# Weights of all gemms split by two GpSimd loads, one rounding and one adding, in place of one SyncE load, a ScalarE rounding and a VectorE subtraction

## The chip, the cores and the metric

One core of one Trainium2 chip runs the whole program. The metric is the device time of one execution in microseconds (us); lower is better. The engines are TensorE (PE, its weight loads PEld), VectorE (DVE), ScalarE (ACT), GpSimd (POOL) and SyncE (SP). SP, ACT and POOL can issue DMA transfers; all of these run on the core's 16 DMA engines.

## The reference, cut to what matters

Two blocks run on 512 tokens of width 1024 in fp32. The first has two layers (a mixer of two linear recurrences, then a gated feed-forward with a convolution), the second one layer (four mixers, then an MLP).

```python
def first_block(x, ...):
    for l in range(DEPTH):                      # 2 layers
        h = _rmsnorm(x, mix_norm[l])
        x = x + _mixer(h, w_in[l], ..., w_branch_dn[l], w_branch_hg[l], w_out[l])
        h = _rmsnorm(x, ffn_norm[l])
        x = x + _conv_ffn(h, w_up[l], ffn_conv[l], ffn_conv_bias[l], w_down[l])
    return _rmsnorm(x, final_norm)

def _mixer(h, w_in, ...):
    p = h @ w_in                                # 1024 x 6672
    ...                                         # gated delta rule and HGRN2, 4 heads each, both directions
    merged = (jax.nn.sigmoid(gate_dn) * (o_dn @ w_branch_dn)
              + jax.nn.sigmoid(gate_hg) * (o_hg @ w_branch_hg))
    return merged @ w_out

def _conv_ffn(h, w_up, ffn_conv, ffn_conv_bias, w_down):
    gate, up = _split(h @ w_up, (D_FF, D_FF))   # D_FF = 2816
    gate = _dwconv(gate, ffn_conv) + ffn_conv_bias
    return (jax.nn.silu(gate) * up) @ w_down

def second_block(x, ...):                       # one layer
    ...
    mixed = jnp.sum(gates * proj, axis=2)       # gates: 1024 x 4096, proj: four branches 256 x 1024
    x = x + jnp.einsum('bsd,de->bse', mixed, w_out[l])
    hn = _rms(x, norm2_g[l])
    hid = jnp.square(jax.nn.relu(jnp.einsum('bsd,df->bsf', hn, w_mlp1[l])))   # 1024 x 4096
    x = x + jnp.einsum('bsf,fd->bsd', hid, w_mlp2[l])
    return x
```

## The kernel before

Activations are kept with features on the partitions, tokens (512) along the row. Every product with a weight matrix goes through `gemm` (L264). Weights lie in HBM in blocks of 128 output columns; a block of 8 chunks of 128 inputs is a tile [128, 8, 128], 512 KB. To keep fp32 precision with matmuls on fp32r operands (a float format of the same size with a rounded mantissa), both operands are split into a rounded high half and a low half: the product is hi·xh + hi·xl + lo·xh, three matmuls of 128x512 for each chunk, so 24 for a block, added up in one PSUM bank `pd` (two banks).

`weights` (L235) makes the halves. SP loads the raw block `wr` (L244, three buffers), ACT writes its rounding `wh` (L245, two buffers), DVE writes `wl` = raw - hi (L246, two buffers). `mm3` (L249) issues the three matmuls of a chunk (L257). The activation's halves `xh`, `xl` are made by `split` (L276).

The order on each engine is written by a scheduler that plays the program through a model of its times; what comes out is a fixed order on each engine, with semaphore waits between engines. In the first block's mixers (`mixer`, L718) the gemms of `w_in` are mixed with the recurrences of the heads: `gdn_front`, `gdn_inverse`, `gdn_scan` (L435 to L612), and `hg_head` (L631), whose loop over seven doublings runs over PE (`ph`, L682), DVE (`att` L684, `qk` L686) and POOL (`pq` L687). After them come the branch products and `w_out` (L774 on), the feed-forward (`ffn`, L784: 44 blocks of `w_up`, of which every second one is followed by a POOL product `fs` L803, then 8 gemms of 22 chunks with `w_down`), and in the second block `mixer2` (L1084) and `mlp` (L1129). POOL carries elementwise work of the recurrences and eight small transfers (`k2`, L961, L962); it issues no weight loads.

Of the kernel before, what the change touches and what calls it, by code (L numbers as in the profile page):

```python
# [17 lines left out]
P = 128  # L18
# [155 lines left out]
class Net:  # L174
# [59 lines left out]

    def weights(self, src, lo="v", small=None):  # L235
        nc = self.nc
        n, c = src.shape[1], src.shape[2]
        pl, k, bf = (self.wp, 8, (3, 2, 2)) if small is None else (small, 2, (2, 2, 2))
        raw, hi, lw = (pl.tile([P, k, P], dt, name=self.nmx(t), tag=t, bufs=b) for t, dt, b in zip(("wr", "wh", "wl"), (F32, F32R, F32R), bf))
        if c == P:  # L240
            raw, hi, lw = raw[:, :n], hi[:, :n], lw[:, :n]
        else:
            raw, hi, lw = (t.rearrange("p a b -> p (a b)")[:, :n * c].rearrange("p (a b) -> p a b", b=c) for t in (raw, hi, lw))
        nc.sync.dma_start(raw, src)  # L244
        nc.scalar.activation(hi, raw, AF.Copy)  # L245
        (nc.vector if lo == "v" else nc.gpsimd).tensor_tensor(lw, raw, hi.bitcast(F32), op=ALU.subtract)  # L246
        return hi, lw
# [6 lines left out]
    def mm(self, *a, **k):  # L254
        """a matmul; those of a paced stretch are queued behind the steps of a scan, a few after each"""
        if not self.pace:
            return self.nc.tensor.matmul(*a, **k)  # L257
        with self.tc.issue_after(self.pace[0]):
            self.nc.tensor.matmul(*a, **k)  # L259
        self.paced += 1  # L260
        if self.paced % PACE == 0:
            self.pace.pop(0)

    def gemm(self, srcs, xs, lo="v", m=P):  # L264
        bank = self.bank("pd")
        ps = bank[:m]
        nk = sum(s.shape[1] for s in srcs)
        k = 0
        for s in srcs:
            hi, lw = self.weights(s, lo)  # L270
            for i in range(s.shape[1]):
                self.mm3(ps, hi[:, i], lw[:, i], xs[k][0], xs[k][1], k == 0, k == nk - 1)
                k += 1
        return bank
# [52 lines left out]
    def norm2_end(self, st):  # L327
        """the final norm of the first block and the first of the second in one"""
        nc = self.nc
# [67 lines left out]
    def gdn_small(self, l, xs, rb, sp):  # L397
        """token-major gates of all heads: columns (c, d*4+h)"""
        nc = self.nc
# [77 lines left out]
    @staticmethod  # L477
    def pair(t, width, b, first, off, n):
        """columns off .. off + n of a tile [P, 2 * width], blocks of b taken in turn from its halves, from half `first` at the start"""
        return bass.AP(tensor=t.tensor, offset=t.offset + off + first * width, ap=[list(t.ap[0]), [2 * b, n // (2 * b)], [b + (1 - 2 * first) * width, 2], [1, b]])  # L480
# [340 lines left out]
    def gemm_tok(self, w, xs, n, rb, pool, tmp, tag):  # L821
        """a bank [tokens, 4, n]"""
        t = self.evac(self.gemm([w], xs, m=n)[:n], rb[:n], pool, *tmp, part=n)
# [5 lines left out]
    def fold_final(self):  # L829
        """fin * norm1 gains, used while the last FFN of the first block leaves"""  # L830
        self.fg = self.cp.tile([P, KD], F32, name="fg1")
        self.nc.vector.tensor_tensor(self.fg, self.col("fin", 0, 8), self.col("n1", 0, 8), op=ALU.mult)
# [321 lines left out]
def place_tables(nc):  # L1154
    """Loads of activation tables, each for the longest run of functions that one set serves"""
    from concourse.hw_specs import get_activation_tables
# [63 lines left out]
```

## Time and profile before

| | |
|---|---|
| three runs | 2740.33, 2744.57, 2746.9 us; median 2744.57 us |
| profiled execution | span 2742.3 us from the first to the last instruction; its own time is not listed apart from the span |
| busy share of the span | PE 96%, PEld 79%, DVE 57%, ACT 41%, POOL 12% |
| mean granted TensorE clock | 0.983 of full speed |
| HBM read | 238.36 MB, of which the weights by SP's queue 215.17 MB |
| weight blocks | 449 loads by SP; 449 ACT roundings; 449 DVE subtractions |

The span is the time on the chip between the first and the last instruction. A busy share is a mean over stages that differ; a PE that is busy may still run below its full rate, since the ends of matmuls are modelled.

### The profile page before, as it was taken

The page shows a single profiled execution, that of the slowest core. Times are in us where ns is not written, and L with a number is a line of the kernel's source. Part 1 is how long each engine was busy: PE and PEld are TensorE (multiplying, and loading weights), DVE is VectorE, ACT ScalarE, POOL GpSimd, SP SyncE. Part 2 cuts the span into 40 slices and gives each one's busy share as a digit, 9 for nine tenths or more (in the row PEclk, how much of TensorE's full clock was granted, in tenths as well). Part 3 has the DMA queues.
Part 4 walks back from the last instruction along what each step waited for, and adds up shares of the span by engine and source line. Part 5 has one row for each costly group of instructions (what it writes and reads, how often), then busy time and mean ns, then how long its engine had stood idle before and what let it go on. Part 6 is the DMA issues. An engine that isn't in the chain of part 4 may idle for free.

```text
span 2742.3 us, 32455 instructions
## 1 busy us (share of the span) xinstructions
PE 2645.3 (96%) x12674; PEld 2178.6 (79%) x12674; DVE 1556.6 (57%) x2234; ACT 1124.7 (41%) x1511; POOL 329.2 (12%) x282
## 2 busy tenths in 40 slices
PE   7999899999999979998999999999999999999999
PEld 4788788878888857887888788888777788888887
DVE  6778764455554366778644555534874444553442
ACT  6545544343333255455443433333446443332221
POOL 1112320001110011122200011100100111000000
PEclk9999989999999999999999999999999999999999
DMA  4112212253223332111123423234411232433332
GB/s 149 62 49 67 62 39 68 88 167 100 94 98 114 121 89 70 55 61 54 39 76 101 160 95 100 93 121 127 145 64 51 82 96 94 140 129 99 94 104 88
DMA packets 99064, 254.13 MB, mean 93 GB/s; under 512 B 10016, under 2 KB 31520, under 8 KB 98656
## 3 DMA queue, kind: packets, MB, share of 16 engines
q1 hardware_dynamic: 66960, 215.17, 24.5%
q10 hardware_dynamic: 31568, 35.85, 4.5%
q8 instruction: 100, 1.64, 0.2%
q0 software_dynamic: 384, 1.05, 0.1%
q14 instruction: 52, 0.43, 0.1%
HBM read 238.36 MB, written 12.62 MB: 92 GB/s over the span
## 4 chain that ended last, share of the span: by engine, by line
PE 49%; ACT 1%; DVE 0%; issue 0%; POOL 0%; ACTq 0%; DVEq 0%; POOLq 0%
PE pd L257 45%; PE ph L1065 1%; PE pl L1053 1%; PE pd L259 1%; ACT wh L245 0%; PE pr L1061 0%; ACT L1179 0%; PE pl L972 0%; PE ph L682 0%; PE pl L843 0%; DVE wl L246 0%; ACT rb L294 0%; ACT rb L295 0%; PE pl L1015 0%; PE ph L1039 0%
## 5 line engine op out<-in xcount | busy, mean ns | idle before, releaser
L257 PE MATMUL pd<-xh,wh 128*128 128x512 f32 (+1 forms) x3186 | 1265.8, 398 | 36.3 <-DVE raw L449 14.3
L257 PE MATMUL pd<-xh,wl 128*128 128x512 f32 (+1 forms) x3188 | 1258.0, 395 | 2.6 <-DVE wl L246 2.3
L257 PE MATMUL pd<-xl,wh 128*128 128x512 f32 (+1 forms) x3186 | 1253.7, 394 | 2.1 <-DVE xl L290 2.0
L245 ACT ACTIVATE wh<-wr 128x1024 fp32r<-128x1024 f32 (+5 forms) x449 | 434.9, 969 | 1011.3 <-PE pd L257 866.8
L257 PEld LDWEIGHTS pd<-xh,wh 128*128 128x128 f32 (+1 forms) x3186 | 600.2, 188 | 178.8 <-issue 20.9
L257 PEld LDWEIGHTS pd<-xl,wh 128*128 128x128 f32 (+1 forms) x3186 | 600.3, 188 | 139.2 <-issue 7.2
L257 PEld LDWEIGHTS pd<-xh,wl 128*128 128x128 f32 (+1 forms) x3188 | 600.0, 188 | 138.7 <-DVE wl L246 5.0
L246 DVE TENSOR_TENSOR wl<-wr,wh 128x1024 fp32r<-128x1024 f32 (+5 forms) x449 | 521.7, 1162 | 250.3 <-ACT wh L245 244.1
L1179 ACT ACT_TABLE_LOAD x116 | 148.8, 1283 | 8.7 <-issue 4.4
L394 DVE TENSOR_TENSOR g<-pd,rb 128x512 f32<-128x512 f32 x64 | 44.3, 692 | 158.2 <-PE pd L257 148.1
L803 POOL TENSOR_TENSOR fs<-fs,rb 128x512 f32<-128x512 f32 x44 | 56.9, 1294 | 506.3 <-ACT fs L802 506.3
L682 PE MATMUL ph<-pq,kc 128*128 128x128 f32 x448 | 74.8, 313 | 19.6 <-POOL er L569 6.7
L797 DVE TENSOR_TENSOR fg<-pd,rb 128x512 f32<-128x512 f32 x44 | 30.5, 693 | 109.9 <-PE pd L257 107.0
L682 PEld LDWEIGHTS ph<-pq,kc 128*128 128x128 f32 x448 | 66.7, 213 | 26.4 <-issue 19.2
L687 POOL TENSOR_TENSOR pq<-pq,f 128x512 f32<-128x512 f32 x48 | 58.8, 1225 | 230.7 <-PE ph L682 211.5
L805 DVE TENSOR_TENSOR fs<-fs,pd 128x512 f32<-128x512 f32 x44 | 30.3, 688 | 90.0 <-POOL fs L803 90.0
L801 DVE SCALAR_TENSOR_TENSOR fs<-fg,cv,fs 128x512 f32<-128x512 f32 x88 | 65.9, 749 | 3.6 <-ACT fs L799 1.9
L802 ACT ACTIVATE fs<-fs 128x512 f32<-128x512 f32 x44 | 27.8, 632 | 85.5 <-DVE fs L801 85.5
L394 DVE TENSOR_TENSOR mh<-pd,rb 128x512 f32<-128x512 f32 x32 | 22.1, 692 | 70.2 <-PE pd L257 68.8
L680 ACT COPY kc<-qk 128x512 f32<-128x512 f32 x56 | 36.9, 659 | 52.2 <-PE ph L682 44.5
L454 DVE SCALAR_TENSOR_TENSOR qk<-raw,cv,qk 128x512 f32<-128x512 f32 x64 | 54.1, 858 | 2.6 <-ACT qk L452 2.2
L684 DVE COPY_PREDICATED att<-um,ph 128x512 f32<-128x512 uint8 x56 | 41.2, 736 | 21.5 <-PE ph L682 21.2
(332 smaller groups left out, 2442.5 us busy)
## 6 DMA issues: line engine op xcount, KB each, us to landing
wr<-in_w_in_dram SPq DMA_DIRECT2D x126, 512.0 KB, 3.3
wr<-in_w_up_dram SPq DMA_DIRECT2D x88, 512.0 KB, 3.3
wr<-in_w_m_dram SPq DMA_DIRECT2D x64, 512.0 KB, 3.8
wr<-in_w_dn_dram SPq DMA_DIRECT2D x32, 512.0 KB, 3.6
wr<-in_w_gt_dram SPq DMA_DIRECT2D x32, 512.0 KB, 3.3
wr<-in_w_out_dram SPq DMA_DIRECT2D x24, 512.0 KB, 3.4
xd<-xn ACTq DMA_DIRECT2D x40, 256.0 KB, 2.0
xo<-xd ACTq DMA_DIRECT2D x32, 256.0 KB, 2.8
```

What stands on the lines that cost most here:

```text
L245: nc.scalar.activation(hi, raw, AF.Copy)
L246: (nc.vector if lo == "v" else nc.gpsimd).tensor_tensor(lw, raw, hi.bitcast(F32), op=ALU.subtract)
L257: return self.nc.tensor.matmul(*a, **k)
L394: self.nc.vector.tensor_tensor(out, ps, rb, op=ALU.mult)
L454: V.scalar_tensor_tensor(o, raw[:, j:j + T], self.col(f"dnc{l}_{j}", ch), o, op0=ALU.mult, op1=ALU.add)
L680: A.copy(kc.rearrange("p (n e b) -> p n e b", e=2, b=hh), self.pair(qk, T, hh, 0, 0, T))
L682: PE.matmul(pl[:, c], kc[:, c * P:(c + 1) * P], self.pair(pq, T, hh, 1, c * P, P), start=True, stop=True)
L684: V.copy_predicated(att, self.um[:, o:o + P].unsqueeze(1).to_broadcast([P, 4, P]), pl)
L687: (G if hh > 1 else V).tensor_tensor(halves(pq, hh, True), halves(pq, hh, True), tot(F, n, 0, n + 1, hh), op=ALU.mult)
L801: nc.vector.scalar_tensor_tensor(g, gp[:, j:j + T], self.col(f"fc{l}_{j}", m), g, op0=ALU.mult, op1=ALU.add)
L803: nc.gpsimd.tensor_tensor(g, g, rb, op=ALU.mult)
L1179: nc.scalar.preload_act_table_set(s)
```

## The change

The high half is loaded by GpSimd straight into the fp32r tile `wh` (four buffers), so that the transfer rounds. ACT writes its negative into `wl` (three buffers), and a second GpSimd transfer of the same block adds the raw weights to it: -hi + raw. The raw tile, SP's load and the DVE subtraction go. In `gemm`, the 16 matmuls of a block that use the high half come first, then the 8 of the low half. The small weights of the second block's branches (`small`, two chunks) get three buffers each and keep the old order of matmuls.

```diff
-    def weights(self, src, lo="v", small=None):
+    def weights(self, src, small=None):
...
-        pl, k, bf = (self.wp, 8, (3, 2, 2)) if small is None else (small, 2, (2, 2, 2))
-        raw, hi, lw = (pl.tile([P, k, P], dt, name=self.nmx(t), tag=t, bufs=b) for t, dt, b in zip(("wr", "wh", "wl"), (F32, F32R, F32R), bf))
+        pl, k, bf = (self.wp, 8, (4, 3)) if small is None else (small, 2, (3, 3))
+        hi, lw = (pl.tile([P, k, P], F32R, name=self.nmx(t), tag=t, bufs=b) for t, b in zip(("wh", "wl"), bf))
...
-        nc.sync.dma_start(raw, src)
-        nc.scalar.activation(hi, raw, AF.Copy)
-        (nc.vector if lo == "v" else nc.gpsimd).tensor_tensor(lw, raw, hi.bitcast(F32), op=ALU.subtract)
+        nc.gpsimd.dma_start(hi, src)
+        nc.scalar.activation(lw, hi.bitcast(F32), AF.Copy, scale=-1.0)
+        nc.gpsimd.dma_start(lw, src, accum_op=ALU.add)
         return hi, lw
...
-        for s in srcs:
-            hi, lw = self.weights(s, lo)
-            for i in range(s.shape[1]):
-                self.mm3(ps, hi[:, i], lw[:, i], xs[k][0], xs[k][1], k == 0, k == nk - 1)
-                k += 1
+        for j, s in enumerate(srcs):
+            hi, lw = self.weights(s)
+            n = s.shape[1]
+            for i in range(n):
+                self.mm(ps, hi[:, i], xs[k + i][0], start=j == 0 and i == 0, stop=False)
+                self.mm(ps, hi[:, i], xs[k + i][1], start=False, stop=False)
+            for i in range(n):
+                self.mm(ps, lw[:, i], xs[k + i][0], start=False, stop=j == len(srcs) - 1 and i == n - 1)
+            k += n
```

On POOL, in the first head's doubling loop in the first mixer, the order before has the six products `pq` one after the other (what a row waits for stands in brackets):

```order
L687 TENSOR_TENSOR pq_768<-pq_768,f_159_923 128x2x128x2 [waits DVE_49,PE_49]
L687 TENSOR_TENSOR pq_768<-pq_768,f_766 128x2x64x4 [waits DVE_49,PE_49,Pool_49]
L687 TENSOR_TENSOR pq_768<-pq_768,f_159_923 128x2x32x8 [waits DVE_49,PE_49,Pool_49]
L687 TENSOR_TENSOR pq_768<-pq_768,f_766 128x2x16x16 [waits DVE_49,PE_49,Pool_49]
L687 TENSOR_TENSOR pq_768<-pq_768,f_159_923 128x2x8x32 [waits DVE_49,PE_49,Pool_49]
L687 TENSOR_TENSOR pq_768<-pq_768,f_766 128x2x4x64 [waits DVE_49,PE_49,Pool_49]
```

The same place of the changed program (the line of `pq` is now L691; L245 is the rounding load, L247 the adding one):

```order
L691 TENSOR_TENSOR pq_761<-pq_761,f_148_912 128x2x128x2 [waits DVE_49,PE_49]
L245 DMA wh_1594<-in_w_in_dram 128x1024 [waits DMASW3_49,PE_49]
L691 TENSOR_TENSOR pq_761<-pq_761,f_759 128x2x64x4 [waits DVE_49,PE_49,Pool_49]
L247 DMA wl_1558<-in_w_in_dram 128x1024 [waits DMASW6_49,Activation_49]
L245 DMA wh_1627<-in_w_in_dram 128x1024 [waits DMASW5_49,PE_49]
L691 TENSOR_TENSOR pq_761<-pq_761,f_148_912 128x2x32x8 [waits DVE_49,PE_49,Pool_49]
L247 DMA wl_1595<-in_w_in_dram 128x1024 [waits DMASW0_49,Activation_49]
L691 TENSOR_TENSOR pq_761<-pq_761,f_759 128x2x16x16 [waits DVE_49,PE_49,Pool_49]
L245 DMA wh_1791<-in_w_in_dram 128x1024 [waits DMASW7_49,PE_49]
L691 TENSOR_TENSOR pq_761<-pq_761,f_148_912 128x2x8x32 [waits DVE_49,PE_49,Pool_49]
L247 DMA wl_1628<-in_w_in_dram 128x1024 [waits DMASW2_49,Activation_49]
L691 TENSOR_TENSOR pq_761<-pq_761,f_759 128x2x4x64 [waits DVE_49,PE_49,Pool_49]
```

Three loads of each kind now stand between these products; a load of `wh` waits for PE (its buffer), one of `wl` for ACT (the negative).

On POOL in the first layer's `w_up`, the order before holds only the products `fs`, one for two blocks:

```order
L803 TENSOR_TENSOR fs_4726<-fs_4726,rb_4673 128x512 [waits Activation_49]
L803 TENSOR_TENSOR fs_4800<-fs_4800,rb_4673 128x512 [waits Activation_49]
L803 TENSOR_TENSOR fs_4874<-fs_4874,rb_4673 128x512 [waits Activation_49]
L803 TENSOR_TENSOR fs_4948<-fs_4948,rb_4673 128x512 [waits Activation_49]
L803 TENSOR_TENSOR fs_5022<-fs_5022,rb_4673 128x512 [waits Activation_49]
```

The changed program has there (a block's `wl` has the number of its `wh` plus one):

```order
L807 TENSOR_TENSOR fs_4792<-fs_4792,rb_4596 128x512 [waits Activation_49]
L247 DMA wl_4907<-in_w_up_dram 128x1024 [waits DMASW6_49,Activation_49]
L245 DMA wh_4978<-in_w_up_dram 128x1024 [waits DMASW5_49,PE_49]
L247 DMA wl_4944<-in_w_up_dram 128x1024 [waits DMASW0_49,Activation_49]
L245 DMA wh_5015<-in_w_up_dram 128x1024 [waits DMASW7_49,PE_49]
L807 TENSOR_TENSOR fs_4864<-fs_4864,rb_4596 128x512 [waits Activation_49]
L247 DMA wl_4979<-in_w_up_dram 128x1024 [waits DMASW2_49,Activation_49]
```

The adding load of a block stands one place behind the rounding load of the next block, and four loads stand between two products.

On PE in the same stretch, the order before alternates the halves within each chunk:

```order
L257 MATMUL pd_5176<-xh_4494,wh_5178 128x512
L257 MATMUL pd_5176<-xl_4495,wh_5178 128x512
L257 MATMUL pd_5176<-xh_4494,wl_5179 128x512
L257 MATMUL pd_5176<-xh_4537,wh_5178 128x512
L257 MATMUL pd_5176<-xl_4538,wh_5178 128x512
L257 MATMUL pd_5176<-xh_4537,wl_5179 128x512
```

The changed order, at the place in a block where its low half begins:

```order
L258 MATMUL pd_5086<-xl_4548,wh_5087 128x512
L258 MATMUL pd_5086<-xh_4589,wh_5087 128x512
L258 MATMUL pd_5086<-xl_4590,wh_5087 128x512
L258 MATMUL pd_5086<-xh_4297,wl_5088 128x512 [waits DMASW6_49]
L258 MATMUL pd_5086<-xh_4337,wl_5088 128x512
L258 MATMUL pd_5086<-xh_4379,wl_5088 128x512
```

The first low-half matmul moved from third to seventeenth in its block and waits for the adding load itself; the number of matmuls is the same.

## Rows read from the trace of the kernel before

**Rows 1.** The page: span, then busy time, share and instructions of each engine.

```profile
span 2742.3 us, 32455 instructions
PE 2645.3 (96%) x12674; PEld 2178.6 (79%) x12674; DVE 1556.6 (57%) x2234; ACT 1124.7 (41%) x1511; POOL 329.2 (12%) x282
```

**Rows 2.** Busy time by stretch, columns as headed: two mixers, one feed-forward's `w_up`.

```profile
core 0: us, PE busy (x) PEld busy (x) DVE busy (x) ACT busy (x) POOL busy (x), PEclk, DMA share, GB/s
0.00:450.00 450.00, 405.31 (x2224) 340.19 (x2225) 319.57 (x531) 235.70 (x320) 91.92 (x83) 0.95 0.22 68
...
605.00:843.00 238.00, 237.50 (x1045) 195.69 (x1044) 126.09 (x152) 92.48 (x113) 28.47 (x22) 1.00 0.30 97
...
1000.00:1400.00 400.00, 360.24 (x2054) 310.29 (x2054) 289.45 (x458) 198.86 (x266) 90.83 (x67) 0.94 0.19 57
```

**Rows 3.** What PE waited for, 0 to 450: total us, times, longest.

```profile
PE ph L698 <- DVE att L684: 4.4, 2, 3.4
...
PE ph L682 <- POOL er L569: 3.5, 1, 3.5
...
PE pd L257 <- DVE wl L246: 0.3, 1, 0.3
```

**Rows 4.** What PE waited for, 1000 to 1400.

```profile
PE pd L257 <- DVE raw L449: 10.4, 1, 10.4
...
PE ph L682 <- POOL er L569: 3.2, 1, 3.2
...
PE pr L589 <- DVE zf L550: 0.4, 1, 0.4
```

**Rows 5.** Groups by line over the whole span: busy, mean ns, idle before.

```profile
L245 ACT ACTIVATE wh<-wr 128x1024 fp32r<-128x1024 f32 (+5 forms) x449 | 434.9, 969 | 1011.3 <-PE pd L257 866.8
...
L246 DVE TENSOR_TENSOR wl<-wr,wh 128x1024 fp32r<-128x1024 f32 (+5 forms) x449 | 521.7, 1162 | 250.3 <-ACT wh L245 244.1
```

**Rows 6.** DVE's group of subtractions, 0 to 450, then 1000 to 1400.

```profile
L246 DVE TENSOR_TENSOR wl<-wr,wh 128x1024 fp32r<-128x1024 f32 x42 | 53.7, 1279 | 8.3 <-ACT wh L245 8.2
...
L246 DVE TENSOR_TENSOR wl<-wr,wh 128x1024 fp32r<-128x1024 f32 x37 | 49.7, 1344 | 3.3 <-ACT wh L245 3.2
```

**Rows 7.** DVE in order of time, 1008 to 1017: start, duration.

```profile
1011.94 1.21 DVE L246 TENSOR_TENSOR wl<-wr,wh 128x1024 fp32r<-128x1024 f32 x1
...
1013.68 1.21 DVE L246 TENSOR_TENSOR wl<-wr,wh 128x1024 fp32r<-128x1024 f32 x1
```

**Rows 8.** ACT's group of roundings, 605 to 843.

```profile
L245 ACT ACTIVATE wh<-wr 128x1024 fp32r<-128x1024 f32 x44 | 46.7, 1061 | 99.2 <-PE pd L257 95.6 <-issue 3.6
```

**Rows 9.** DMA, 605 to 843: SP's queue (packets, MB, share); issues with us to landing.

```profile
q1 hardware_dynamic: 6316, 22.86, 29.8%
...
wr<-in_w_up_dram SPq DMA_DIRECT2D x39, 512.0 KB, 3.3
```

**Rows 10.** DMA queues of SP (q1) and ACT (q10), 560 to 605 (`w_out`).

```profile
q1 hardware_dynamic: 1172, 4.28, 29.2%
q10 hardware_dynamic: 2304, 4.20, 29.1%
```

**Rows 11.** The same, 2350 to 2395.

```profile
q1 hardware_dynamic: 1150, 4.19, 28.4%
q10 hardware_dynamic: 2016, 3.67, 24.1%
```

**Rows 12.** POOL's own transfers: issue in ns (min, median, max); size and us to landing.

```profile
L961 POOL DMA_DIRECT2D k<-tn x4: 518/518/687, 1953.3 to 1963.8; - x4
...
k<-tn POOLq DMA_DIRECT2D x4, 128.0 KB, 2.9
```

**Rows 13.** The line of `pq` (L687): its durations, and who waited for it.

```profile
L687 POOL TENSOR_TENSOR pq<-pq,f x48: 1048/1118/2096, 125.9 to 1359.6; 128x512 f32<-128x512 f32 x48
...
  PEld ph L682: 11.6, 10
  PE ph L682: 6.9, 10
```

More of the change, by code (lines that the diff above doesn't have):

```diff
@@ L233, in bank @@
         return self.pm.tile(list(shape), F32, name=self.nmx(tag), tag=tag, bufs=self.nb[tag])
-    def weights(self, src, lo="v", small=None):
+    def weights(self, src, small=None):
         nc = self.nc
         n, c = src.shape[1], src.shape[2]
-        pl, k, bf = (self.wp, 8, (3, 2, 2)) if small is None else (small, 2, (2, 2, 2))
-        raw, hi, lw = (pl.tile([P, k, P], dt, name=self.nmx(t), tag=t, bufs=b) for t, dt, b in zip(("wr", "wh", "wl"), (F32, F32R, F32R), bf))
+        pl, k, bf = (self.wp, 8, (4, 3)) if small is None else (small, 2, (3, 3))
+        hi, lw = (pl.tile([P, k, P], F32R, name=self.nmx(t), tag=t, bufs=b) for t, b in zip(("wh", "wl"), bf))
         if c == P:
-            raw, hi, lw = raw[:, :n], hi[:, :n], lw[:, :n]
+            hi, lw = hi[:, :n], lw[:, :n]
         else:
-            raw, hi, lw = (t.rearrange("p a b -> p (a b)")[:, :n * c].rearrange("p (a b) -> p a b", b=c) for t in (raw, hi, lw))
-        nc.sync.dma_start(raw, src)
-        nc.scalar.activation(hi, raw, AF.Copy)
-        (nc.vector if lo == "v" else nc.gpsimd).tensor_tensor(lw, raw, hi.bitcast(F32), op=ALU.subtract)
+            hi, lw = (t.rearrange("p a b -> p (a b)")[:, :n * c].rearrange("p (a b) -> p a b", b=c) for t in (hi, lw))
+        nc.gpsimd.dma_start(hi, src)
+        nc.scalar.activation(lw, hi.bitcast(F32), AF.Copy, scale=-1.0)
+        nc.gpsimd.dma_start(lw, src, accum_op=ALU.add)
         return hi, lw
@@ L262, in mm, with gemm @@
             self.pace.pop(0)
-    def gemm(self, srcs, xs, lo="v", m=P):
+    def gemm(self, srcs, xs, m=P):
         bank = self.bank("pd")
         ps = bank[:m]
-        nk = sum(s.shape[1] for s in srcs)
         k = 0
-        for s in srcs:
-            hi, lw = self.weights(s, lo)
-            for i in range(s.shape[1]):
-                self.mm3(ps, hi[:, i], lw[:, i], xs[k][0], xs[k][1], k == 0, k == nk - 1)
-                k += 1
+        for j, s in enumerate(srcs):
[7 more added lines that the diff above has]
+            k += n
         return bank
```

## The prediction, made before the result was known

> **What bounds the kernel now.** The page's busy times come first: TensorE (PE) is busy for 2645.3 of 2742.3 us, and nothing else comes near [rows 1]. All idle time of PE together is 97 us, so nothing that leaves its matmuls alone can win more than 97 us plus what a higher clock gives back. Next comes the table by stretch, to see where these 97 us lie [rows 2]. In the feed-forward (605 to 843) PE is busy for 237.5 of 238 us at a granted clock of 1.00. In the two mixers' recurrences (0 to 450, 1000 to 1400) it is busy for 405.3 and 360.2 us, idle for 45 and 40 us, and the clock granted is 0.95 and 0.94, a mean of its levels 2.4 and 1.2 GHz. So 85 of the 97 us lie in 850 us of mixers; the other 1892 us are matmuls end to end.
>
> Who is waited for in the mixers stands in PE's waits. From 0 to 450, 12 rows name DVE, the first 4.4 us, the last 0.3; they sum to 24.8 us [rows 3]. From 1000 to 1400, 10 rows from 10.4 down to 0.4 sum to 29.5 us [rows 4]. POOL's rows are short (its longest 3.5 and 3.2). DVE is the engine to relieve, in the mixers only.
>
> **DVE's subtraction goes.** It is 449 instructions, 521.7 us [rows 5]. Outside the mixers PE does not wait for DVE, and what it frees there is worth nothing. In the mixers the subtractions are 53.7 of 319.6 and 49.7 of 289.5 us of DVE's work [rows 2, 6], 17%. The longest wait, 10.4 us for `raw` [rows 4], ends after two of them on DVE, 1.21 us each [rows 7]. That is 2.4 of 10.4 us, or 23%, so the share of 17% is a fair measure of all: 0.17 x 54.3 = 9 us. Bounds: nothing, and half of the waits (27 us). Term: **-9 us**.
>
> **ACT's rounding becomes a negation** of the same tile from the same size: 449 instructions at 969 ns both times [rows 5]. No change of time. ACT's long wait for PE (866.8 us) stays in kind, since it now waits for a `wl` buffer.
>
> **The matmuls** are as many as before. Reordering high before low gives the low half more time and costs nothing that I can see in a row.
>
> **Does the supply hold in the feed-forward?** A block takes 238 / 44 = 5.41 us on PE [rows 2, 8], 3.61 for the 16 high-half matmuls, 1.80 for the 8 low ones. With three `wl` buffers, ACT can negate block n+3 once block n is done, and the low half of n+3 is due 2 x 5.41 + 3.61 = 14.4 us later. The way there: ACT 1.06 us [rows 8], the issue on POOL, and the landing. POOL's own transfers, of half the partitions and half the row, issue in 0.52 us and land in 2.9 us [rows 12]; SP's 512 KB land in 3.3 us [rows 9]. The issue I bound by 0.52 us and four times that (twice the rows, twice the operands), and take 1.04 us. The landing of the adding load I bound by 3.3 us and three times that. Even 1.06 + 2.07 + 9.9 = 13.0 us is under 14.4. POOL's time is there too: 2 x 1.04 us each block beside half a product `fs`. So latency does not stop PE; only the rate of the DMA engines could.
>
> **The rate.** SP's queue took 29.8% of 238 us for 22.86 MB [rows 9], 43.6 blocks: 1.63 us of all 16 engines for one. No row shows a rounding or an adding load. The rounding load moves the same bytes: bounds 1.63 us and twice that (if reading and writing don't overlap); I take 1.63, since a transfer of a like size from POOL lands as fast as one from SP [rows 9, 12]. The adding load must read its destination as well: bounds 1.63 us (the second read hidden) and 4.89 (two reads and a write in turn); I take 3.26. Sum 4.89 us of 5.41, 90%. The supply holds, closely. Where activations move too, it does not: from 560 to 605 the weights' 29.2% times three plus ACT's 29.1% is 117% [rows 10], 7.5 us too much; the same stretch of the second layer (1512 to 1555) I count alike; 2350 to 2395 gives 109%, 4 us [rows 11]. Of these 19 us the loads that stand four blocks ahead (21.6 us of matmuls) cover about half. Bounds 0 and 19; term: **+10 us**.
>
> By the Trainium skill (Collectives: The Full Stack, section "The bandwidth ceiling: the fold count and why AG ≠ RS ≠ AR") an addition inside the DMA engines costs no cycles of its own, but needs two source reads in one queue and so runs at half a copy's rate. By that the adding load stays at 3.26 us and this term at +10; with the lower end of the rows the term would be nothing. No run so far shows such a load.
>
> **POOL in the mixers.** It now issues about two loads for each of some 45 blocks in each mixer, and works its queue in order. A product `pq` behind a load of `wh` waits until PE has freed that buffer, one behind a load of `wl` until ACT has negated, and then for the issue. In the piece of the order shown, five of six products `pq` have a load just ahead. Behind `pq` stands the next level's matmul on PE: PE already waits for `pq` 20 times, 18.5 us in all [rows 13]. In those places there is no slack, and 5/6 of them pay one issue: 20 x 5/6 x 1.04 = 17 us. Bounds: nothing (POOL is busy for 92 of 450 us [rows 2]), and a landing of 3.3 us for each of the 20, 66 us. Term: **+17 us**.
>
> **Sum.** 2742.3 - 9 + 10 + 17 = 2760 us of span. The median of the runs shown is 2744.57, 2.3 us above the span; with that, **2763 us**, 0.7% slower.
>
> **Rivals.**
> *Faster: the mixers gain.* DVE's backlog breaks, half of the waits for it go (-27 us), and the clock climbs half of the way to 1.00 there, 0.025 x 405 + 0.03 x 360 = 21 us. POOL's loads cost nothing, since most of its products are not waited for. 2742.3 - 48 + 2.3 = 2697 us. For it: DVE is busy for 71% of the mixers. Against: ACT, PE and the chains between them set most of those waits too.
> *No change.* DVE's gain and POOL's cost cancel: about 2745 us. The change does what it says, and PE does not care.
> *Slower: the DMA engines become the bound.* Place: every stretch of matmuls end to end, 1892 us. It decides from the point where rounding plus adding load take more than 5.41 us; I count 4.89, so 0.5 us is the margin. With the adding load at 4.89 the block takes 6.52 us, and 1892 x (6.52 / 5.41 - 1) = 388 us: some 3130 us. With both at their upper ends (3.26 + 4.89 = 8.15) some 3700. For it: the margin is 10%, and neither load has a row. Against: SP's queue is busy only 30% of the time now.
>
> **How the numbers follow.** A run of this kernel tells about 0.2% (5.5 us) from no change. Chances: the forecast (slower by 0.2 to 2%) 0.37; faster 0.27; within 0.2% 0.11; DMA bound (over 2%) 0.25. So faster 0.27, same 0.11, slower 0.62. The range goes from 2690 us (a little beyond the faster rival) up to 2980 us, where the two loads take about 6.1 us a block; outside it I leave 0.04 below and 0.16 above. The likeliest case alone spans 2750 to 2800: 0 to 19 us for the DMA engines, 0 to 66 for POOL.
>
> **What would show it.** Right: in the profile after, PE still at 237 of 238 us in `w_up`, the DMA share there near 0.9, DVE down by some 520 us, waits of PE for `pq` longer in the mixers, and PE waiting for `wl` near `w_out`. Wrong: PE waiting for DMA in `w_up`, or matmul counts of a 50 us slice falling there (then the loads are slower than I took them, and the adding load's landing says which); or PE's idle time in the mixers falling below 60 us with POOL's products on time (then the relief of DVE was worth more than a share of the waits). A rounding load that takes more of the DMA engines than 1.63 us would break the choice of the lower bound.

## The result, and the profile after

The changed kernel takes 2770.8 us (median of 4 runs, 2762.6 to 2773.3) against 2742.5 us of the kernel before on the same chip: ratio 1.0099, 95% interval 1.0079 to 1.0120, so 28 us or 1.0% slower. The profiled execution took 2768.7 us, its span is 2766.9.

The head of its page answers to [rows 1]:

```profile
span 2766.9 us, 32672 instructions
...
PE 2647.2 (96%) x12674; PEld 2175.1 (79%) x12674; DVE 1082.6 (39%) x1785; ACT 1120.0 (40%) x1511; POOL 953.5 (34%) x1180
```

PE has the same instructions and, within 2 us, the same busy time. DVE has lost its 449 subtractions and 474 us (less than the 521.7 of [rows 5], mostly because the records of neighbouring instructions overlap and the page counts the overlap once); POOL has 898 issues more and three times its busy time. The span is 24.6 us longer, and PE's busy time grew by 2: the rest is idle time of PE.

Busy time by stretch, the same stretches as in [rows 2]:

```profile
core 0: us, PE busy (x) PEld busy (x) DVE busy (x) ACT busy (x) POOL busy (x), PEclk, DMA share, GB/s
0.00:450.00 450.00, 404.03 (x2235) 337.43 (x2236) 275.42 (x489) 235.53 (x323) 152.32 (x173) 0.96 0.52 118
605.00:843.00 238.00, 235.91 (x1037) 194.25 (x1036) 78.61 (x110) 93.84 (x115) 89.37 (x108) 1.00 0.87 195
1000.00:1400.00 400.00, 364.29 (x2069) 311.84 (x2068) 248.46 (x421) 200.64 (x267) 137.95 (x139) 0.94 0.49 106
```

`w_up` holds: PE 235.9 of 238 us, at a DMA share of 0.87. In the recurrences DVE works 41 to 44 us less, and PE's busy time there has hardly moved (404 and 364 us, before 405 and 360). So no net relief reached PE there, and the loss lies elsewhere. DMA, 605 to 843, answers to [rows 9]:

```profile
q0 software_dynamic: 12678, 46.03, 86.5%
...
wl<-in_w_up_dram POOLq DMA_DIRECT2D x42, 512.0 KB, 5.5
wh<-in_w_up_dram POOLq DMA_DIRECT2D x40, 512.0 KB, 4.2
```

46.03 MB are 43.9 blocks, each loaded twice: 0.865 x 238 / 43.9 = 4.69 us of all 16 DMA engines for a block's two loads, where the prediction had 4.89. In `w_out` of the first layer, against [rows 10], the queues of POOL and ACT together fill the engines (98.8%):

```profile
q0 software_dynamic: 2184, 7.95, 73.9%
q10 hardware_dynamic: 2146, 3.91, 24.9%
```

Where the 28 us arise is read by laying DVE's products of both traces side by side: the start of the same product in the other kernel, less its start in the kernel before. From here on, the first and second mixer are those of the two layers, the third is the mixer of the second block. The table holds the kernels of the experiments too; each column is one profiled execution, in us.

| up to here | after | order_only | no_sub | no_add | half_add | pool_plain | ws_dve | br_old | m2_old |
|---|---|---|---|---|---|---|---|---|---|
| first recurrences done | -1.3 | +13.7 | -13.1 | -2.5 | +2.6 | -0.7 | +2.7 | +2.3 | +0.5 |
| `w_out`, layer 1 | +2.5 | +13.7 | -14.8 | -2.5 | +1.0 | +0.7 | +4.0 | +1.2 | +1.5 |
| second recurrences done | +4.0 | +22.8 | -25.2 | -11.6 | -8.2 | +5.9 | +1.6 | +4.8 | +2.4 |
| `w_dn`, layer 2 | +2.3 | +22.3 | -26.7 | -12.7 | -10.9 | +7.3 | +3.3 | +4.8 | +3.9 |
| third mixer, first 8 gates | +8.0 | +25.6 | -31.3 | -8.9 | -2.8 | +12.1 | +3.6 | +15.4 | +12.1 |
| the other 24 gates | +18.4 | +28.0 | -31.5 | -9.8 | -4.1 | +13.0 | +16.2 | +15.2 | +11.8 |
| `w_out` of the third mixer | +24.5 | +27.5 | -31.4 | -10.5 | -2.8 | +14.1 | +21.3 | +20.2 | +11.0 |
| the end | +24.6 | +27.5 | -31.4 | -10.4 | -2.7 | +14.1 | +21.4 | +20.3 | +11.1 |

ws_dve has the changed kernel's order on every engine up to 1930 us, br_old and m2_old up to 1411; yet in the first row these four columns lie between -1.3 and +2.7. A step of less than about 4 us in one column is therefore no finding.

After both layers the changed kernel is 2.3 us behind; the third mixer loses 22 us more, in three places; the MLP, end to end matmuls at a DMA share of 0.88 to 0.92, loses nothing.

**First place, the start of the third mixer.** PE stands still for 11.9 us, where before it waited 3.3 us. All engines in order of time (start, duration, what; in brackets the idle time before, and what ended it):

```profile
1931.96 1.26 POOL L856 TENSOR_TENSOR ws<-ws,cm 128x512 f32<-128x512 f32 x1 [8.44 <-DMA ws<-in_ws_dram]
1933.17 1.14 POOL L245 DMA_DIRECT2D wh<-in_w_in_dram  x2
...
1939.27 1.06 ACT L246 ACTIVATE wl<-wh 128x1024 fp32r<-128x1024 f32 x1 [9.39 <-DMA wh<-in_w_in_dram]
1940.23 0.70 ACT L298 ACTIVATE rb<-rb,biasc 128x512 f32<-128x512 f32 x1
...
1941.63 0.69 DVE L340 TENSOR_TENSOR rb<-rb,rb 128x512 f32<-128x512 f32 x1 [10.23 <-ACT rb L299]
1942.36 0.69 DVE L398 TENSOR_TENSOR tc<-pd,rb 128x512 f32<-128x512 f32 x1
1943.10 0.79 PE L258 MATMUL pd<-xh,wh 128*128 128x512 f32 x1 [11.91 <-DVE tc L398]
```

POOL waits 8.4 us for a small load (`ws`); two rounding loads stand behind that product in its queue; ACT waits 9.4 us for the landing of one; the norm factor `rb` stands behind that negation on ACT, `tc` behind `rb` on DVE, and PE needs the bank that `tc` empties. PE's row names DVE, but the chain begins in POOL's queue. Before, the same product waited as long, but had no load of weights behind it:

```profile
1925.12 2.32 POOL L852 TENSOR_TENSOR ws<-ws,cm 128x512 f32<-128x512 f32 x1 [8.22 <-DMA bs<-in_bs_dram]
```

**Second place, the 24 later gates.** PE waits from 2160 to 2370:

```profile
PE pd L258 <- DVE g L398: 7.2, 3, 5.5
```

and what ACT waits for, 2197 to 2370:

```profile
ACT wl L246 <- DMA wh<-in_w_br_dram: 27.2, 7, 6.2
```

Before, ACT's rounding waited for PE above all [rows 5]. Now its negation waits for a landing for up to 6.2 us, and behind it in ACT's queue `xh`, for which DVE's `xl` and then `g` wait. The longest wait of PE in order of time:

```profile
2309.27 0.89 POOL L247 DMA_DIRECT2D wl<-in_w_br_dram  x1 [3.93 <-ACT wl L246]
...
2310.39 0.88 POOL L245 DMA_DIRECT2D wh<-in_w_br_dram  x1
...
2316.21 0.42 ACT L246 ACTIVATE wl<-wh 128x256 fp32r<-128x256 f32 x1 [5.68 <-issue]
2316.53 0.61 ACT L290 ACTIVATE xh<-acc 128x512 fp32r<-128x512 f32 x1
...
2317.18 0.69 DVE L291 TENSOR_TENSOR xl<-acc,xh 128x512 fp32r<-128x512 f32 x1 [5.93 <-ACT xh L290]
...
2317.79 0.68 DVE L398 TENSOR_TENSOR g<-pd,rb 128x512 f32<-128x512 f32 x1
...
2318.52 0.80 PE L258 MATMUL pd<-xh,wh 128*128 128x512 f32 x1 [5.55 <-DVE g L398]
```

The rounding load issued at 2310.39 lands at 2316.14, so it is what ACT waits for at 2316.21, though the row names nothing ("issue"). The rows close a loop: the rounding load of the next branch block stands in POOL's queue behind the adding load of the last one, which waits for ACT's negation, which waits for the landing of the rounding load before. From 2261 to 2316 eight negations in a row start within 0.15 us of that landing, 7.8 us apart on average; a gate and its branch block took 6.8 us before. The waits of PE in the 24 gates make up 7 us of the 10 lost. The other 3 us PE works at a lower clock: in the stretch that holds this wait, 266 matmuls take 63.4 us at a granted clock of 0.95, a mean of its levels of 2.4 and 1.2 GHz (first row, the changed kernel); 265 took 60.0 us at 1.00 (second row, before; columns as above).

```profile
2260.00:2330.00 70.00, 63.41 (x266) 50.99 (x265) 13.71 (x20) 19.18 (x29) 36.08 (x44) 0.95 0.82 170
...
2252.00:2312.00 60.00, 60.00 (x265) 49.61 (x265) 27.04 (x38) 19.30 (x29) 11.66 (x9) 1.00 0.29 91
```

**Third place**, `w_out` of the third mixer, 6 us, where the two queues share the DMA engines as in [rows 11]; from 2370 to 2410 they reach 0.98. PE does not wait for weights there. It waits for `xn`, and DVE before it for the activations that ACT's queue brings back (19.5 us, before 5.6; window 2365 to 2430):

```profile
PE pd L258 <- DVE xn L1128: 2.5, 2, 1.8
...
DVE xo L1125 <- DMA xo<-xd: 19.5, 6, 5.6
```

### The profile page after: what moved, and what is told of

The parts are those of the page before. It is cut to its first block, busy times and chain, and to the rows that moved or that the text cites. A ratio compares the mean times of both kernels' runs of the same rounds, so it can differ in the third digit from the quotient of the medians.

```text
span 2766.9 us, 32672 instructions
## 1 busy us (share of the span) xinstructions
PE 2647.2 (96%) x12674; PEld 2175.1 (79%) x12674; DVE 1082.6 (39%) x1785; ACT 1120.0 (40%) x1511; POOL 953.5 (34%) x1180
## 4 chain that ended last, share of the span: by engine, by line
PE 43%; issue 4%; POOL 2%; DMA 1%; ACT 1%; DVE 0%; ACTq 0%; POOLq 0%; DVEq 0%
PE pd L258 39%; POOL wh L245 1%; POOL acc L1109 1%; POOL wl L247 1%; DMA xo<-xd 1%; PE ph L1069 1%; PE pd L260 1%; PE pl L1057 0%; PE pr L1065 0%; DMA wl<-in_w_out_dram 0%; PE pl L976 0%; DMA wh<-in_w_in_dram 0%; ACT xh L290 0%; PE ph L686 0%; PE pl L847 0%
## 5 line engine op out<-in xcount | busy, mean ns | idle before, releaser
L258 PE MATMUL pd<-xh,wh 128*128 128x512 f32 (+2 forms) x3184 | 1263.8, 398 | 52.7 <-DVE raw L453 13.5
L258 PE MATMUL pd<-xl,wh 128*128 128x512 f32 (+2 forms) x3184 | 1255.8, 395 | 2.4 <-DVE xl L294 2.2
L246 ACT ACTIVATE wl<-wh 128x1024 fp32r<-128x1024 f32 (+4 forms) x449 | 434.5, 969 | 1070.6 <-PE pd L258 800.7
L258 PE MATMUL pd<-xh,wl 128*128 128x512 f32 (+1 forms) x3192 | 832.5, 395 | 0.7 <-DMA wl<-in_w_out_dram 0.7
L258 PEld LDWEIGHTS pd<-xh,wh 128*128 128x128 f32 (+2 forms) x3184 | 601.8, 189 | 197.2 <-DVE raw L453 17.1
L258 PEld LDWEIGHTS pd<-xl,wh 128*128 128x128 f32 (+2 forms) x3184 | 602.2, 189 | 138.0 <-DVE xl L294 5.6
L247 POOL DMA_DIRECT2D wl<-in_w_in_dram x126 | 109.3, 868 | 319.5 <-ACT wl L246 301.3
L245 POOL DMA_DIRECT2D wh<-in_w_in_dram x126 | 77.1, 613 | 242.0 <-PE pd L258 202.7
L1183 ACT ACT_TABLE_LOAD x116 | 148.8, 1283 | 21.3 <-issue 18.4
L247 POOL DMA_DIRECT2D wl<-in_w_up_dram x88 | 76.1, 865 | 159.1 <-ACT wl L246 155.8
L247 POOL DMA_DIRECT2D wl<-in_w_m_dram x64 | 54.5, 851 | 159.1 <-ACT wl L246 155.8
L398 DVE TENSOR_TENSOR g<-pd,rb 128x512 f32<-128x512 f32 x64 | 44.1, 690 | 140.9 <-PE pd L258 129.8
L245 POOL DMA_DIRECT2D wh<-in_w_up_dram x88 | 51.6, 586 | 133.3 <-PE pd L258 128.0
L686 PE MATMUL ph<-pq,kc 128*128 128x128 f32 x448 | 70.3, 302 | 14.8 <-DVE att L688 9.4
L820 DVE TENSOR_TENSOR xn<-pd,xo 128x512 f32<-128x512 f32 x16 | 11.1, 692 | 186.2 <-PE pd L258 186.2
L686 PEld LDWEIGHTS ph<-pq,kc 128*128 128x128 f32 x448 | 63.4, 204 | 23.2 <-issue 15.8
L691 POOL TENSOR_TENSOR pq<-pq,f 128x512 f32<-128x512 f32 x48 | 55.1, 1147 | 73.9 <-issue 35.9
L247 POOL DMA_DIRECT2D wl<-in_w_dn_dram x48 | 41.1, 856 | 99.5 <-ACT wl L246 96.9
```

The costliest lines, as they stand in the source:

```text
L245: nc.gpsimd.dma_start(hi, src)
L246: nc.scalar.activation(lw, hi.bitcast(F32), AF.Copy, scale=-1.0)
L247: nc.gpsimd.dma_start(lw, src, accum_op=ALU.add)
L398: self.nc.vector.tensor_tensor(out, ps, rb, op=ALU.mult)
L686: PE.matmul(pl[:, c], kc[:, c * P:(c + 1) * P], self.pair(pq, T, hh, 1, c * P, P), start=True, stop=True)
L691: (G if hh > 1 else V).tensor_tensor(halves(pq, hh, True), halves(pq, hh, True), tot(F, n, 0, n + 1, hh), op=ALU.mult)
```

## The experiments

Each kernel was timed beside the kernel before, and its ratio is to that. Theory A puts the loss into queues that work in order, theory B into the rate of the DMA engines, theory C into the order of the matmuls.

One thing holds for all of them: the scheduler writes the whole order anew for each kernel, and not only at the place of the edit. Of DVE's 1785 instructions other than subtractions (counted from the traces, by their tiles' names), all keep their order against the changed kernel in ws_dve, 1769 in br_old, 1742 in m2_old, 1709 in no_add and half_add, 1638 in after_old_order. Against the kernel before only 1535 to 1548 do in the changed kernel, order_only, no_sub and pool_plain, 1518 in sub_pool, 1476 and 1487 in the two mixed kernels. So ws_dve and br_old show their one edit; the prices of no_sub, order_only, pool_plain, sub_pool and the mixed kernels are those of an edit together with a new order on DVE, and no run holds that order fixed.

**ws_dve.** One product leaves POOL's queue.

```diff
-        G.tensor_tensor(ws, ws, self.mk("tri_f")...)
+        V.tensor_tensor(ws, ws, self.mk("tri_f")...)
```

> The changed kernel with one product moved: `ws` times the triangle mask at the start of the third mixer goes from POOL to DVE, so that it no longer stands in POOL's queue ahead of the loads of weights. Theory A (queues: POOL works its queue in order, so a load behind a product that waits is late, and ACT behind that load is late too): the 8.4 us lost at the third mixer's start come back, 2771 becomes about 2762. Theory B (rate: the DMA engines are near full there, 0.91, and would be so anyway): 2771, within 3 us. The prediction's theory (POOL's issues stand ahead of `pq` in the first two mixers): no change either.

Measured: 2765.5 us, ratio 1.0085 (1.0069 to 1.0100), 5 us less than the changed kernel. The first 8 gates now lose 0.3 us instead of 5.7 (table), and the wait is this:

```profile
PE pd L258 <- DVE tc L398: 4.9, 1, 4.9
```

The chain through POOL's queue is shown for this place: 11.9 us became 4.9, with nothing else moved on DVE, ACT or POOL. The other two places stay. The total came down less than expected, and within the spread of both kernels' runs.

**br_old.** The 32 blocks of `w2_br` alone come by the old way.

```diff
+        if small is not None:
+            raw = ...
+            nc.sync.dma_start(raw, src)
+            nc.scalar.activation(hi, raw, AF.Copy)
+            nc.vector.tensor_tensor(lw, raw, hi.bitcast(F32), op=ALU.subtract)
+            return hi, lw
```

> The changed kernel, but the 32 blocks of w2_br alone (128 KB each) come by the old way: SP's plain load, ACT's rounding, DVE's subtraction. Theory A: in the gate and branch phase ACT waits for the landing of `wh` of w_br (42 us in 15 waits of the whole run), and PE behind it for `g`; with the old way the 11 us lost in this phase come back, 2771 becomes about 2760. Theory B: the phase's DMA share falls from 0.85 by a tenth or so, and about a third of the 11 us comes back: 2767. The prediction's theory: 2771.

Measured: 2763.3 us, ratio 1.0065 (1.0053 to 1.0078). The 24 gates lose nothing now (+15.4 to +15.2), where the changed kernel lost 10.4 us; the third mixer's start lost 5 us more in this profile, so a part went back. The place is shown. Whether it is ACT's wait or the bytes, this run does not tell: both go.

**m2_old.** All blocks of the third mixer by the old way, through two raw tiles in a pool that this mixer opens (`if self.old:` in place of `if small is not None:`).

> The changed kernel, but every block of the third mixer (w2_in, w2_gt, w2_br, w2_out) comes by the old way, through two raw tiles of its own; the two first layers and the last MLP keep the new way. By the offsets of the trace after (about 2 us lost in both first layers, 25 in the third mixer, none in the MLP) it should stand at about 2746: theories A and B alike, since both put the loss into this mixer. The prediction's theory, with its loss in the first two mixers (17 us) and a part of 10 us at w_out: not below 2765.

Measured: 2761.1 us, ratio 1.0063 (1.0050 to 1.0077): neither number. Gates and `w_out` lose nothing (+12.1 to +11.0), as A and B said, but the start loses 8 us, by a fault of the experiment: the pool of raw tiles opens with the mixer, SP's first load there is issued at 1927.7, after the layer's last matmul (1920), and PE waits for it through ACT:

```profile
PE pd L266 <- ACT wh L250: 5.1, 1, 5.1
```

**no_add.** The adding load is left out, so the low half is only minus the high half.

```diff
-        nc.gpsimd.dma_start(lw, src, accum_op=ALU.add)
```

> The changed kernel without the adding load: the low half is only the negative of the high half, so the output is not the reference's (the second load of every block and its sum are left out). Half of POOL's issues and about two thirds of the DMA engines' time go. Theory B (rate): all of the loss comes back, 2742 or a little less, and the DMA share in w_up falls from 0.87 to about 0.3. Theory A: the product `ws` still holds up the rounding loads and ACT still waits in order for their landings, so at least the 8 us at the third mixer's start stay: 2752 to 2762. The prediction's theory: half of the 17 us for POOL's issues and all of the 10 us for the DMA engines come back: 2752.

Measured: 2735.4 us, ratio 0.9968 (0.9955 to 0.9980): 35 us less than the changed kernel, and 10 less than before; A's 2752 to 2762 and the prediction's 2752 fail, B's 2742 or a little less is nearest. So the adding load alone costs more than the whole loss. As A said, the wait at the third mixer's start stays (8.4 us, behind `ws`); as B said, the rest goes. This run also prices the rounding load by itself, 605 to 843:

```profile
q0 software_dynamic: 6336, 22.94, 32.6%
...
wh<-in_w_up_dram POOLq DMA_DIRECT2D x40, 512.0 KB, 3.6
```

22.94 MB are 43.8 blocks: 0.326 x 238 / 43.8 = 1.77 us for one, so 4.69 - 1.77 = 2.92 us are the adding load's.

**half_add.** The adding load covers half of the block: as many issues by POOL, fewer bytes. (Half of the low halves is left out.)

```diff
-        nc.gpsimd.dma_start(lw, src, accum_op=ALU.add)
+        h = n // 2
+        nc.gpsimd.dma_start(lw[:, :h], src[:, :h], accum_op=ALU.add)
```

> The changed kernel, but each adding load covers only the first half of its block, so the output is not the reference's (half of the low halves is left out). POOL issues as many loads as in the change; the DMA engines' time for a block falls from 4.7 us to about 3.2 (1.77 for the rounding load, measured without the adding load, and half of the 2.92 that are left). Theory B (rate): the losses in the gate and branch phase and at w_out go, 25 or more of the 35 us that the full removal gave back: 2745 or less. Theory A (queues, number of issues): less than 8 us come back, 2763 or more.

Measured: 2747.4 us, ratio 1.0008 (0.9998 to 1.0019): 23 of the 35 us come back with the number of issues unchanged; by the table (its profile is 6 us below the median) 12 in the 24 gates, 11 in the second recurrences, 5 at each `w_out` of the first and third mixer (the 4 us that the first recurrences lose are no more than equal programs differ by). So two thirds of the adding load's cost follow its bytes, not POOL's queue. In the second recurrences the DMA share of the changed kernel is 0.49, so full engines are not the way there; that it is the landing of single loads (5.5 us for `wl` of `w_in` in the changed kernel, 4.1 here) is argued, not shown. The 12 us that are left are POOL's issues or the other half of the bytes. In `w_up` a block's two loads now take 64.5% of 238 us for 43.3 blocks, 3.55 us: half an adding load costs 1.8, more than half of 2.92. Of the two expectations, B's 2745 or less is nearer to 2747 than A's 2763 or more.

**order_only.** The kernel before, with the matmul order of the change alone.

```diff
-            for i in range(s.shape[1]):
-                self.mm3(ps, hi[:, i], lw[:, i], xs[k][0], xs[k][1], ...)
+            for i in range(n):
+                self.mm(ps, hi[:, i], xs[k + i][0], ...)
+                self.mm(ps, hi[:, i], xs[k + i][1], ...)
+            for i in range(n):
+                self.mm(ps, lw[:, i], xs[k + i][0], ...)
```

> The kernel before with one part of the change alone: in each group of weights all high-half matmuls come first, then the low-half ones; loads, rounding and subtraction stay as they were. The prediction counted this part at nothing: 2745, within 3 us. A rival: the low half has more time after its subtraction, PE's short waits for `wl` in the mixers go, and some us are won: 2735 to 2742.

Measured: 2771.7 us, ratio 1.0102 (1.0089 to 1.0116), and both expectations fail: 29 us slower, in the profile 14, 9 and 5 us in the three mixers. DVE in order of time before the longest new wait:

```profile
61.89 2.79 DVE L506 SCALAR_TENSOR_TENSOR gb<-gb,gs,cm 128x128 f32<-128x128 f32 x4 [1.12 <-DMA gb<-gd]
64.61 0.68 DVE L470 TENSOR_TENSOR qk<-qk,raw 128x512 f32<-128x512 f32 x1
65.21 3.14 DVE L506 SCALAR_TENSOR_TENSOR gb<-gb,gs,cm 128x128 f32<-128x128 f32 x4
68.28 1.21 DVE L246 TENSOR_TENSOR wl<-wr,wh 128x1024 fp32r<-128x1024 f32 x1
69.41 0.68 DVE L452 TENSOR_TENSOR raw<-pd,rb 128x512 f32<-128x512 f32 x1
```

PE's matmul at 70.14 waited 12.35 us for that `raw`: the matmuls that filled the banks were done by 56 us, and DVE's queue held two groups of `gb` and a subtraction ahead of the evacuation. Before, one group of `gb` stood just ahead of it, and PE waited 3.9 us. The order of the matmuls is written in the code; the place of the evacuation in DVE's queue follows from it when the program is built.

**no_sub.** The kernel before without the subtraction; the high half stands in for the low one.

```diff
-        (nc.vector if lo == "v" else nc.gpsimd).tensor_tensor(lw, raw, hi.bitcast(F32), op=ALU.subtract)
-        return hi, lw
+        return hi, hi
```

> The kernel before without DVE's subtraction of the low half: the high half stands in for it in the third matmul, so the output is not the reference's (the low half is left out, PE's work is the same). It measures the relief of DVE alone. The prediction's term: 9 us won, in the first two mixers, 2736. Rival (the relief is worth much more, and the change hid it behind a larger loss): 27 us or more, 2718 or less. Rival (the waits that name DVE are chains through it, not its load): nothing, 2745.

Measured: 2718.0 us, ratio 0.9909 (0.9893 to 0.9924). Without the subtraction, and with the order written for that, 24 us of the median are won (31 in the profile: 15, 12 and 5 in the three mixers): near the prediction's upper bound of 27, not its 9. PE's longest wait, for `raw` in the second recurrences, does not go: 10.4 us [rows 4] become 8.6, at 995.6 us instead of 1015.6. In the first, 3.9 us become 1.3. Before, 0 to 450, then no_sub, 0 to 450 and 950 to 1400:

```profile
PE pd L257 <- DVE raw L449: 3.9, 1, 3.9
...
PE pd L256 <- DVE raw L448: 1.3, 1, 1.3
...
PE pd L256 <- DVE raw L448: 8.6, 1, 8.6
```

The gain is thus spread over smaller waits: in the profile PE's idle time up to the end of the first recurrences falls from 44.5 to 31.7 us, and in the second, from the end of the first feed-forward on, from 40.0 to 29.6.

**pool_plain.** The kernel before; POOL issues each block's plain load in two halves.

```diff
-        nc.sync.dma_start(raw, src)
+        h = n // 2
+        nc.gpsimd.dma_start(raw[:, :h], src[:, :h])
+        nc.gpsimd.dma_start(raw[:, h:], src[:, h:])
```

> The kernel before, but each block's plain load is issued by POOL as two halves instead of once by SP: as many issues in POOL's queue as the change has (two a block), and the DMA engines move the same bytes as before (share about 0.30 in w_up). The prediction's theory (POOL's issues stand ahead of its products in the first two mixers): 17 us lost there, 2762 in all. Theory A (queues): a loss at the third mixer's start, about 8 us, and part of the 11 us in the gate and branch phase, 2753 to 2762, little in the first two mixers. Theory B (rate of the DMA engines): 2745, within 4 us.

Measured: 2758.0 us, ratio 1.0049 (1.0037 to 1.0062): 15.5 us for POOL's issues with the order written for them, against rate theory B. The size is that of the prediction's term, the place is not: nothing in the first recurrences, 5 us in the second, 5 at the third mixer's start, 2 in the gates and `w_out`. Each of these steps is hardly more than equal programs differ by; the sum is clear.

**after_old_order.** The changed kernel with the old order of matmuls (the reverse of the diff of order_only).

> The changed kernel with the matmuls back in the old order (for each row of blocks: high with xh, high with xl, low with xh); loads and negation stay new. Theory C (the new order costs by itself, since it moves DVE's evacuations behind other work, as it did by 29 us in the old kernel): most of these come back, 2741 to 2755. Rival (with the adding load the low half lands late, and the old order needs it 3.6 us sooner, so PE waits for `wl`): 2771 to 2800.

Measured: 2816.2 us, ratio 1.0266 (1.0250 to 1.0283): 45 us slower than the changed kernel. Theory C falls for the new kernel. The rival holds, by more than it said: PE now waits for the low half's landing,

```profile
PE pd L258 <- DMA wl<-in_w_in_dram: 18.4, 10, 3.1
...
PE pd L258 <- DMA wl<-in_w_out_dram: 12.3, 5, 3.3
```

where the changed kernel has 0.7 us of it. The new order is what makes the adding load bearable.

**mix_new, mix_new_oo.** The new loads only where DVE was waited for (`w_in` in the first two recurrences), the old way elsewhere, with three `wh` (one fewer than the change has), three `wl` and two raw buffers; the second with the old matmul order.

```diff
+        if not self.new:            # set only around the recurrences
+            raw = ...
+            nc.sync.dma_start(raw, src)
+            nc.scalar.activation(hi, raw, AF.Copy)
+            nc.vector.tensor_tensor(lw, raw, hi.bitcast(F32), op=ALU.subtract)
+            return hi, lw
```

> Both ways in one kernel: the rounding and adding loads only for w_in in the recurrences of the first two mixers, where DVE is waited for; everywhere else SP's plain load, ACT's rounding and DVE's subtraction; high-half matmuls first everywhere. With the rate theory the losses outside the first two mixers go: about 2740 (the changed kernel stood about 2 us ahead to 3 us behind in these stages). Theory C (the order costs in the mixers whatever the loads are): 2745 to 2765, since the order then also costs in the third mixer, where the old way is back.

> As the kernel with both ways (new loads for w_in in the first two recurrences alone), but with the old matmul order everywhere. Theory C with the relief of DVE at its measured worth (27 us in these two mixers without any subtraction) and POOL's issues at theirs (6 us): 2720 to 2728, ahead of both kernels. Rival (the low half lands too late for the old order): no gain, 2745 or more.

Measured: 2777.7 us (ratio 1.0140, 1.0123 to 1.0157) and 2761.0 us (1.0066, 1.0053 to 1.0078). Both are slower than the kernel before. The new order costs 17 us here, as in the old kernel and unlike in the changed one. With the old order, the first two recurrences still lose 5 and 4 us (each near what equal programs differ by), instead of winning 27: PE waits 10.3 and 9.7 us for `raw`. So in these kernels, even where DVE's relief is worth most, the loads that pay for it take more; whether the missing buffer or the new order on DVE has a part in that was not tried apart.

**sub_pool.** The kernel before; in the first two recurrences POOL subtracts in DVE's place.

```diff
-        (nc.vector if lo == "v" else nc.gpsimd).tensor_tensor(lw, raw, ...)
+        (nc.gpsimd if self.new else nc.vector).tensor_tensor(lw, raw, ...)
```

> The kernel before with DVE relieved in another way: for w_in in the recurrences of the first two mixers alone, POOL does the subtraction of the low half (about 2.4 us each by POOL's product of the same size, some 45 in each mixer); loads, rounding and matmul order stay as before, and no load goes through POOL. If DVE's relief is the whole story there (27 us measured without any subtraction in these two mixers): 2718 to 2730, ahead of both kernels. Rival (POOL's queue again: a subtraction that waits for ACT stands ahead of `pq` and `er`, and takes as long as two of them): 2745 to 2775.

Measured: 2770.9 us, ratio 1.0096 (1.0082 to 1.0110): the rival. The work moved is 2.43 us each:

```profile
L247 POOL TENSOR_TENSOR wl<-wr,wh 128x1024 fp32r<-128x1024 f32 x84 | 204.0, 2429 | 332.2 <-ACT wh L246 303.0 <-DMA gb<-gd 11.3 <-ACT w L593 7.9
```

and the loss (12 and 13 us) lies in the same two recurrences. No version that computes the reference was faster than the kernel before.

## Why the prediction was right in its number, and where its steps were not

The forecast of 2763 us, slower, stands beside 2771. Its three terms, -9, +10 and +17, sum to +18; measured +28. The direction rests on one step that held, the rate in `w_up`. That the size came out near is luck: some terms were off by as much as the whole sum, in both directions. Term by term:

- **The rate held in `w_up`, as worked out.** Rounding load 1.77 us of 16 engines (taken 1.63), adding load 2.92 (taken 3.26), together 4.69 (4.89) of 5.41 us. The rival of a full DMA bound fell with it. The Trainium skill (Collectives: The Full Stack, "The bandwidth ceiling: the fold count and why AG ≠ RS ≠ AR") says of a ReduceScatter that the add needs two source reads and so runs at about half the rate of an AllGather's copy. Here, on one core, 2.92 us against the 1.63 of SP's plain load is 0.56 of its rate: near the rule, and the sum by the rule would have been the same.
- **The stretches at `w_out`: half of the size found, the path another.** +10 was predicted. In the third mixer's the offsets grow by 6.1 us (5.1 in ws_dve, 5.0 in br_old). At the first layer's branches and `w_out` they grow by 3.8, but where ws_dve, m2_old and br_old run the same program there, by 1.3, 1.0 and -1.1. The second's was predicted to be as full, and is (its share reads 1.04 from 1510 to 1555), yet costs nothing. And PE was to wait for `wl` there; in the whole run it does so for 0.7 us. It waits behind ACT and DVE, which wait for landings.
- **The term that failed first: "Reordering high before low ... costs nothing that I can see in a row."** In the old kernel it comes with 29 us, through the order that DVE's queue then gets; in the new one its absence costs 45, through low halves that land too late. It has no price of its own, and the prediction should have read in the order on DVE where the evacuations come to stand.
- **The relief of DVE was mis-sized**: 24 us (31 in the profile) in no_sub, against 9. The share of the subtractions in DVE's work does fit the wait that it was taken from, which fell by 1.8 us of 10.4 (17%). The gain lies in other, smaller waits, and how much of it is the order written anew stays open.
- **POOL's issues: size near, place and way wrong.** 15.5 us in pool_plain, of which 2.2 us are PE's own waits for `pq` (9.1 us, before 6.9). In the changed kernel PE itself waits less for `pq` than before, 2.9 us against 6.9 [rows 13]. The 18.5 us of the prediction added PEld's rows to PE's, though weight loads overlap matmuls. For `w_in` an issue took 0.61 us (rounding) and 0.87 (adding), taken 1.04.

```profile
  PEld ph L686: 15.5, 13
  PE ph L686: 2.9, 6
```

- **What no term held: the third mixer.** 16 of the lost us lie at its start and in its gates, 3 of them by the clock. The prediction looked at POOL's queue for late products; the costly ones were late loads, and behind them ACT, which now waits in order for landings. At the start this is shown by ws_dve; in the gates it is shown that the place (br_old) and the bytes of the adding load (half_add) decide; the loop of negation, issue and landing is read from rows, and fits both.
- **Its signs.** Met: `w_up` at 235.9 of 238 us and a DMA share of 0.87. Not met: DVE down by 474 us instead of 520, no longer waits for `pq`, no waits for `wl` near `w_out` beyond 0.7 us.

The single prices do not add up: relief -24, order +29, issues +15 and the adding load's bytes +23 would be +43, not +28. Each but the last comes with a new order on DVE. That order and adding load work against each other is shown (after_old_order); the rest of the sum stays open. Open too is why the first recurrences gain next to nothing after (1.3 us), of the 13 in no_sub. It isn't the adding load (2.5 us gained without it). With the old order of matmuls the gain is 1.0, but there PE also waits 5.1 us for a low half, so the order is not ruled out. What is left beside it, and was not tried apart, is the rounding load's place in POOL's and ACT's queues, and the place of the evacuation on DVE.

## What to carry to other kernels

Work moved from a compute engine into DMA was paid here in landings and queue places before it was paid in bandwidth: the DMA engines held at 87% in the matmul stretches, and most of the loss came where a load stood behind a waiting product, or a small activation behind a landing. When a change shifts loads onto an in-order queue, list for each stage what waits ahead of the first load, and what stands behind the engine that now waits for it. And price an order of matmuls with the loads that it will meet: the same order came with 29 us of loss with one way of loading and spared 45 with the other. Where a scheduler writes the order, part of every such price may be its new order: compare the order of both kernels before naming a cause. And follow a wait by its instruction, not by a fixed window: in no_sub the longest one had only moved out of the window of the kernel before.

## What the runs showed of the hardware that was not expected

A DVE instruction with its inputs in SBUF is slower while POOL computes. From 60.30 the decay tiles `gb` take DVE 2.18 us for eight; from 63.00 four take 4.75 us, while POOL runs four products of 128x512 (the changed kernel, all engines in order of time):

```profile
60.30 2.18 DVE L507 SCALAR_TENSOR_TENSOR gb<-gb,gs,cm 128x128 f32<-128x128 f32 x8
61.43 0.85 POOL L247 DMA_DIRECT2D wl<-in_w_in_dram  x1 [14.01 <-ACT wl L246]
61.97 0.87 POOL L245 DMA_DIRECT2D wh<-in_w_in_dram  x1
62.40 0.69 DVE L471 TENSOR_TENSOR qk<-qk,raw 128x512 f32<-128x512 f32 x1
62.83 2.23 POOL L510 TENSOR_TENSOR gb<-gb,gs 128x512 f32<-128x512 f32 x2
63.00 4.75 DVE L507 SCALAR_TENSOR_TENSOR gb<-gb,gs,cm 128x128 f32<-128x128 f32 x4
65.03 2.57 POOL L573 TENSOR_TENSOR er<-er,qk 128x512 f32<-128x512 f32 x2
```

That is 0.27 us each beside POOL's issues and 1.19 us each beside its products. The evacuation `raw` stands behind them, and PE's next matmul waits 6.6 us for it. Over the whole run the records of this `gb` group last 345 ns each while POOL does nothing (24 of them), 344 beside its DMA issues (25) and 972 beside its products (15). `g`, which DVE reads from a PSUM bank (L398), lasts 0.69 us each in all three cases (42, 18 and 4). That the one slows the other was read from rows like these, not tried apart. The Trainium skill (SBUF — State Buffer, "SBUF: two separate sides") has a rule for it: VectorE and GpSimd share one pair of ports, which an instruction holds to its end while the other engine stands still; for a VectorE instruction with two inputs in SBUF it holds against a GpSimd one that reads SBUF. The rows agree: a DVE instruction takes about as long there (1.19 us) as the POOL product beside it (1.1 to 1.3).

Rounding in a transfer costs little: 1.77 us of the 16 engines for 512 KB by POOL (no_add, `w_up`), where SP's plain load took 1.63 [rows 9] and POOL's two plain halves 1.51 (pool_plain: 27.5% of 238 us for 43.4 blocks). It landed in 3.6 us, SP's plain load in 3.3.
